# Rows and weight halves of a float32r streaming block at shifting SBUF addresses

## The chip, the cores and the metric

The kernel runs on one NeuronCore of a Trainium2 chip. The metric is the device time of one execution in microseconds (us). Smaller is better.

## What is computed

A residual block over 272 tokens (16 learned ones and 256 of the input), model width 2048, in float32: a feed-forward part, a mixer part and a second feed-forward part, each between two RMSNorms.

```python
h = h + 0.5 * rmsnorm(swiglu(rmsnorm(h, g), w_gate, w_up, w_down), g2)   # 2048 -> 5632 -> 2048
u = rmsnorm(h, mix_pre_g)
z = u @ w_in + b_in                     # 2048 -> 10248 columns: q, k, v, gates, two sigmoid gates
y = sigmoid(gm) * (mlstm(...) @ m_w_branch) + sigmoid(ga) * (diff_attention(...) @ a_w_branch)
h = h + rmsnorm(y @ w_out, mix_post_g)
h = h + 0.5 * rmsnorm(swiglu(...), ...) # the second feed-forward part
return h[:, 16:]                        # the learned tokens are dropped
```

From the queries of the mixers on, only the 256 tokens of the input are carried along; the second feed-forward part works on 256 tokens.

## The kernel before

All weights stream through SBUF once. They lie in DRAM as 377 units (of 128 x 2048 float32, 1 MB); `load_unit` brings one by DMA into a tile `W` (three buffers) and splits it into a high part H, which ACT rounds to float32r, and a low part L = W - H, which DVE writes. H and L come in two halves of 1024 columns, with four buffers each, so two units are held at a time. Tokens are split the same way: the operand of a sub-layer lies in `U`, 16 rows of 576 elements for each partition, the high row first and the low row right behind it at `T` = 272 elements. The hidden activations of a feed-forward part lie in three slots `G0`, `G1`, `G2`.

A matrix product is then three matmuls in float32r, H·XH + H·XL + L·XH, and `product` issues them for one 128 x 128 piece of weights and one row `k`. There are four kinds of units. *Wide* ones work on 272 tokens, as three matmuls of 272 columns (a PSUM bank holds 512). *Narrow* ones work on 256 tokens: H·XH and H·XL go as one matmul of 512 columns whose moving operand is `both`, a pattern of two rows, and L·XH is one of 256. *Cells* are the rows of `G0` to `G2` with 272 tokens in the down projection of the first part, *dense* are those with 256 tokens in the second one and in the two branches. Where `both` is None (the first group of a part, the last block of a tensor that needs it, one of four banks at the end of a down projection), 256 tokens too run as three matmuls.

In products with `both`, `turn` flips from one product to the next, so that the order is both·L, L·both, both·L, L·both; at the first product of a sum it is set back, and the last product always ends with `both`. A kind's units are counted from 0 through the program. `block` runs the 16 rows of one block of 128 output columns; `group` runs four blocks at a time, row by row, over several units. The feed-forward parts are one group and the blocks of gate and up, a down projection over 24 of the 44 hidden blocks, the remaining blocks, and a down projection over the other 20.

Every kind has one fixed pair of starts inside its H and L buffers, in bytes:

```python
PHASES = {"wide": (192, 0), "narrow": (32, 96), "cells": (64, 64), "dense": (192, 192)}
hp, lp = [p // 4 for p in PHASES[kind]]
H = sp.tile([128, 1088], F32R, name="H", bufs=4)[:, hp:hp + 1024]
L = sp.tile([128, 1088], F32R, name="L", bufs=4)[:, lp:lp + 1024]
```

`ROW` is 576 and `CELL` 320 elements. Each engine takes its instructions in the order in which the program is written; nothing is scheduled afterwards. The functions that the diff touches, with the line numbers of the profile:

Of the kernel before, what the change touches and what calls it, by code (L numbers as in the profile page):

```python
# [22 lines left out]
F32R = mybir.dt.float32r  # L23
I32 = mybir.dt.int32
BF16 = mybir.dt.bfloat16
AF = mybir.ActivationFunctionType
OP = mybir.AluOpType
AX = mybir.AxisListType.X

D, SEQ, META, DFF = 2048, 256, 16, 5632  # L30
T = META + SEQ
KT = D // 128
FT = DFF // 128
FA = 24
FB = FT - FA
MH, DQK, DV = 4, 128, 256
AH, ADH, ADV = 8, 64, 128
# [3 lines left out]
ALL, REAL = slice(0, T), slice(META, T)  # L41
# [35 lines left out]
GAPS = (32, 40, 8)  # L77

PHASES = {"wide": (192, 0), "narrow": (32, 96), "cells": (64, 64), "dense": (192, 192)}

@with_exitstack
def block_kernel(ctx: ExitStack, tc: tile.TileContext, ht_d, w_d, vec_d, con_d, gc_d, out_d):
# [10 lines left out]
    def f(ap):  # L98
        return ap.bitcast(F32)
# [4 lines left out]

    hT = cp.tile([128, KT, T], F32, name="hT")
    gap(cp, 0)
    rows = cp.tile([128, KT, ROW], F32R, name="U")
    U = rows[:, :, :2 * T].rearrange("p k (a t) -> p k a t", a=2)
    UH, UL = U[:, :, 0], U[:, :, 1]
    A = cp.tile([128, 4352], F32, name="A")  # L110
    vec = cp.tile([128, NVEC], F32, name="vec")
    con = cp.tile([128, NCON], F32, name="con")
# [5 lines left out]
    def view(t, off, *shape):  # L118
        n = int(np.prod(shape))
        a = t[:, off:off + n]  # L120
        if len(shape) == 1:
            return a
        return a.rearrange("p (a b) -> p a b", a=shape[0])

    def slot(tag, n, dt):
        return gp.tile([128, n], dt, tag=tag, name=tag, bufs=1)

    def v(name, j, n=1):
        o, w = VEC[name]
        return vec[:, o + j:o + j + n]  # L130
# [4 lines left out]

    st = {"pieces": 2}
    unit_no = [0]
    turn = [False]

    def behind(ins, prev):  # L140
        tc.add_manual_dep(ins.ins, prev.ins.name,
                          mybir.DependencyInfo(mybir.DependencyClass.NoSync,
                                               mybir.DependencyReason.DATA), reason="issue order")

    def load_unit(kind, parts=1, hold=None, dma=None):
        pieces = max(parts, st["pieces"])
        u = unit_no[0]
        unit_no[0] += 1
        W = sp.tile([128, 2048], F32, name="W", bufs=3)
        hp, lp = [p // 4 for p in PHASES[kind]]  # L150
        n = 2048 // parts
        for i in range(parts):
            s = slice(i * n, (i + 1) * n)
            st["dma"] = nc.sync.dma_start(W[:, s], w_d[u, :, s])
            if dma:
                dma(i)
        HL = []
        for i in range(2):
            H = sp.tile([128, 1088], F32R, name="H", bufs=4)[:, hp:hp + 1024]
            L = sp.tile([128, 1088], F32R, name="L", bufs=4)[:, lp:lp + 1024]  # L160
            n = 2048 // pieces
            for o in range(0, 1024, n):
                s = slice(o, o + n)
                w = W[:, 1024 * i + o:1024 * i + o + n]
                a = nc.scalar.activation(H[:, s], w, AF.Copy)  # L165
                b = nc.vector.tensor_sub(L[:, s], w, f(H[:, s]))  # L166
                q = (1024 * i + o) // n
                if hold and hold[q % len(hold)]:
                    for x, y in zip((a, b), hold[q % len(hold)]):
                        behind(x, y)  # L170
            HL.append((H, L))
        return HL
# [26 lines left out]
        return tp.tile([128, n], dt, tag=f"s{n}", name=name, bufs=bufs)  # L199

    def product(ps, HL, o, X, first, last):
        turn[0] = False if first else not turn[0]
        H, L = HL[o // 1024]
        o %= 1024
        H, L = H[:, o:o + 128], L[:, o:o + 128]
        XH, XL, both = X
        n = XH.shape[-1]
        if both is None:
            nc.tensor.matmul(ps[:, :n], H, XH, start=first, stop=False)  # L209
            nc.tensor.matmul(ps[:, :n], H, XL, start=False, stop=False)  # L210
            st["mm"] = nc.tensor.matmul(ps[:, :n], L, XH, start=False, stop=last)  # L211
        elif last or turn[0]:
            nc.tensor.matmul(ps[:, :n], L, XH, start=False, stop=False)  # L213
            st["mm"] = nc.tensor.matmul(ps[:, :2 * n], H, both, start=False, stop=last)  # L214
        else:
            nc.tensor.matmul(ps[:, :2 * n], H, both, start=first, stop=False)  # L216
            st["mm"] = nc.tensor.matmul(ps[:, :n], L, XH, start=False, stop=False)  # L217
# [100 lines left out]
        return ps  # L318

    def prenorm_operand(k, g, cols):  # L320
        a = nc.scalar.activation(UH[:, k, cols], hT[:, k, cols], AF.Copy, scale=v(g, k))  # L321
        b = nc.vector.scalar_tensor_tensor(UL[:, k, cols], hT[:, k, cols], v(g, k),  # L322
                                           f(UH[:, k, cols]), op0=OP.mult, op1=OP.subtract)
        return a, b

    def operand(cols):
        return [(UH[:, k, cols], UL[:, k, cols], U[:, k, :, cols]) for k in range(KT)]

    def residual(yg, r, cols, n, g):
        def feed(k):  # L330
# [33 lines left out]
    def ffn(cols, n, post, feed):  # L364
        Y = view(A, 0, KT, n)
        cells, F = [], []
        for tag in SLOTS:
            w = CELL if n > 256 else n
            m = SLOTS[tag] // w if n > 256 else 2 * (SLOTS[tag] // (2 * n))
            t = view(slot(tag, SLOTS[tag], F32R), 0, m, w)  # L370
            cells += [t[:, i, :n] for i in range(m)]
            F += [(t[:, i], t[:, i + 1], t[:, i:i + 2]) for i in range(0, m - 1, 2)]
        X = operand(cols)
        if n > 256:
            F = [(cells[i], cells[FA + i], None) for i in range(FA)]
            X = plain(X)
        state = {}

        def gate(ps):
            t = tmp()  # L380
            times(t[:, :n], ps, state["r"][:, :n])
            nc.scalar.activation(t[:, :n], t[:, :n], AF.Silu)
            return t

        def up(j, sg, ps):
            t = tmp()
            times(t[:, :n], ps, state["r"][:, :n])
            nc.vector.tensor_mul(t[:, :n], t[:, :n], sg[:, :n])
            H, L, _ = F[j % FA]
            nc.scalar.activation(H, t[:, :n], AF.Copy)  # L390
            nc.vector.tensor_sub(L, t[:, :n], f(H))

        def pair(j):
            sg = gate(block(X, 8))
            up(j, sg, block(X, 8))

        def down(chunk, nk):
            for g in range(4):
                last = chunk == 1

                def finish(b, ps):
                    k = 4 * g + b
                    for p in ps:
                        nc.vector.tensor_add(Y[:, k], p, Y[:, k])
                    add_square(state["acc"], Y[:, k], n, k)
                    post_scale(Y, k, post)

                pss = group(F, nk, n, tail=last, after=finish if last else None)
                if not last:
                    for b in range(4):  # L410
                        total(Y[:, 4 * g + b], pss[b])

        psn[0] = 0
        pss = group(X, KT, n, feed=feed)
        pss += [block(X, 8) for _ in range(2)]
        state["r"] = rstd_of(prenorm_sum(cols, n), n, "rpre")
        pss.append(block(X, 8))
        sgs = [gate(pss[0]), gate(pss[1])]
        up(0, sgs[0], pss[2])
        up(1, sgs[1], pss[3])  # L420
        up(2, gate(pss[4]), pss[5])
        up(3, gate(pss[6]), block(X, 8))
        for j in range(4, FA):
            pair(j)
        down(0, FA)
        for j in range(FA, FT):
            pair(j)
        state["acc"] = []
        down(1, FB)
        r = rstd_of(state["acc"], n, "rpost")  # L430
        return Y, r
# [313 lines left out]
    wide = {"mq", "mk", "mv", "ak", "av"}  # L745

    XA, XR = plain(operand(ALL)), operand(REAL)
    waiting, units = [], []

    def start_block(i, cycle=1):  # L750
        full = IN_ORDER[i] == "if" or IN_ORDER[i][0] in wide
# [2 lines left out]
    def begin(g):  # L754
        if g is not None and next(g, "end") != "end":
            waiting.append(g)

    def advance():
        with tc.issue_after(st["mm"].ins):
            for g in list(waiting):  # L760
                if next(g, "end") == "end":
                    waiting.remove(g)
            if units:
                begin(units.pop(0))

    def run(i0, i1):
        for i in range(i0, i1):
# [10 lines left out]
    base = {k: IN_ORDER.index((k, 0)) for k in ("mv", "ak", "gm", "ga")}  # L778
    run(7, base["ak"])
    st["pieces"] = 4  # L780
    units += [mlstm(h, i) for i in range(2) for h in range(MH)]
    run(base["ak"], base["gm"])
    while waiting or units:
        advance()
    st["lam"] = lam()
    units += [attention(h, i) for i in range(2) for h in range(AH)]

    def keep(j, ps):
        total(tm[:, j], ps)
# [1 line left out]
    branch(HM, keep)  # L791
    gz = view(slot("G0", SLOTS["G0"], F32), 0, KT, SEQ)
    run(base["gm"], base["ga"])
    while waiting or units:
        advance()
    st["pieces"] = 2
    for j in range(KT):
# [9 lines left out]
    def merge(j, ps):  # L807
        t = tmp()
        times(t[:, :SEQ], ps, gz[:, j])
        nc.vector.tensor_add(t[:, :SEQ], t[:, :SEQ], tm[:, j])  # L810
        nc.scalar.activation(UH[:, j, REAL], t[:, :SEQ], AF.Copy)
        nc.vector.tensor_sub(UL[:, j, REAL], t[:, :SEQ], f(UH[:, j, REAL]))

    branch(HA, merge)

# [187 lines left out]
```

## Time and profile before

| | before |
|---|---|
| median of the runs | 2274.9 us (2 runs, 2274.74 to 2275.07) |
| profiled execution, its own time | 2273.81 us |
| span of its instructions | 2272.0 us |
| PE busy | 2254.3 us, 99% |
| PE weight loads busy | 2082.1 us, 92% |
| DVE busy | 1419.5 us, 62% |
| ACT busy | 1159.6 us, 51% |
| DMA | 404.56 MB, mean 178 GB/s |

Busy time is the union of an engine's records. Matmuls overlap each other in the records: the next one starts well before the one ahead has ended. So how fast PE goes is read from the distance of starts in the timeline, or from the number of records in a stretch, and not from the mean length of one. Each matmul has a weight load of its own (PEld), also where two in a row use the same weights.

### The profile page before, as it was taken

What the parts mean: (1) busy time and instruction counts of PE and PEld (TensorE: products, weight loads), DVE (VectorE), ACT (ScalarE), POOL (GpSimd) and SP (SyncE); (2) the same over time, 40 slices, a digit from 0 to 9 for tenths busy, and PEclk for the clock granted to TensorE, in tenths of its full rate; (3) what the DMA queues carried; (4) which work ended last, traced back from release to release, by engine and by line L of the source; (5) the groups of instructions that cost most, each with busy time, mean ns of one, the idle gap of its engine ahead of it and who ended that gap; (6) DMA issues with size and microseconds to landing.
All of it is one profiled execution on the core that took longest, in us unless ns stands there. A gap on an engine that the chain in (4) does not pass through costs nothing.

```text
span 2272.0 us, 37068 instructions
## 1 busy us (share of the span) xinstructions
PE 2254.3 (99%) x15325; PEld 2082.1 (92%) x15325; DVE 1419.5 (62%) x2470; ACT 1159.6 (51%) x1869; POOL 0.8 (0%) x5
## 2 busy tenths in 40 slices
PE   9999999999999999999999999999999999999998
PEld 9999999999999998988988888888888888888897
DVE  7555544455555596588588758668666545666655
ACT  6444433444444465555569655556555444545443
POOL 0000000000000000000000000000000000000000
PEclk9999999999999999999999999999999999999999
DMA  7545554554545544434433555545555555555553
GB/s 257 181 179 181 173 185 173 180 180 174 185 171 182 201 158 167 167 131 163 169 135 130 188 195 189 188 167 186 186 185 187 195 194 185 187 193 195 186 185 111
DMA packets 61529, 404.56 MB, mean 178 GB/s; under 512 B 6704, under 2 KB 8880, under 8 KB 14000
## 3 DMA queue, kind: packets, MB, share of 16 engines
q1 hardware_dynamic: 61216, 400.33, 49.6%
q8 instruction: 120, 1.97, 0.3%
q0 software_dynamic: 144, 1.87, 0.2%
q14 instruction: 49, 0.40, 0.0%
HBM read 400.07 MB, written 2.10 MB: 177 GB/s over the span
## 4 chain that ended last, share of the span: by engine, by line
PE 98%; DVE 1%; DMA 0%; ACT 0%; issue 0%; SPq 0%; DVEq 0%
PE mm L214 10%; PE mm L216 10%; PE mm L211 7%; PE mm L209 7%; PE mm L210 7%; PE aux L211 6%; PE aux L209 6%; PE aux L210 6%; PE aux L214 5%; PE aux L216 5%; PE mm L213 5%; PE mm L217 5%; PE aux L213 3%; PE aux L217 3%; PE vt L211 2%; PE vt L209 2%
## 5 line engine op out<-in xcount | busy, mean ns | idle before, releaser
L166 DVE TENSOR_TENSOR L<-W,H 128x1024 fp32r<-128x1024 f32 (+1 forms) x866 | 934.9, 1085 | 597.0 <-ACT H L165 586.6
L165 ACT ACTIVATE H<-W 128x1024 fp32r<-128x1024 f32 (+1 forms) x866 | 811.9, 946 | 751.7 <-PE aux L210 209.3
L209 PE MATMUL mm<-U,H 128*128 128x272 f32 (+1 forms) x1056 | 304.4, 289 | 8.3 <-ACT U L321 7.9
L211 PE MATMUL mm<-U,L 128*128 128x272 f32 (+1 forms) x1056 | 303.6, 288 | 0.4 <-DVE L L166 0.4
L210 PE MATMUL mm<-U,H 128*128 128x272 f32 (+1 forms) x1056 | 302.3, 287 | 0.2 <-DVE U L322 0.2
L216 PE MATMUL mm<-U,H 128*128 128x512 f32 x728 | 288.0, 396 | 0.0
L214 PE MATMUL mm<-U,H 128*128 128x512 f32 x728 | 286.7, 394 | 0.0
L211 PE MATMUL aux<-U,L 128*128 128x272 f32 x752 | 215.8, 287 | 0.0
L209 PE MATMUL aux<-U,H 128*128 128x272 f32 x752 | 214.8, 286 | 0.0
L210 PE MATMUL aux<-U,H 128*128 128x272 f32 x752 | 214.3, 285 | 0.0
L209 PEld LDWEIGHTS mm<-U,H 128*128 128x128 f32 x1056 | 199.5, 189 | 10.3 <-ACT U L321 9.2
L217 PE MATMUL mm<-U,L 128*128 128x256 f32 x728 | 205.6, 282 | 0.0
L213 PE MATMUL mm<-U,L 128*128 128x256 f32 x728 | 203.4, 279 | 0.0
L211 PEld LDWEIGHTS mm<-U,L 128*128 128x128 f32 x1056 | 199.7, 189 | 0.9 <-DVE L L166 0.9
L210 PEld LDWEIGHTS mm<-U,H 128*128 128x128 f32 x1056 | 199.6, 189 | 0.8 <-DVE U L322 0.4
L213 PEld LDWEIGHTS mm<-U,L 128*128 128x128 f32 x728 | 137.1, 188 | 31.5 <-issue 0.4
L217 PEld LDWEIGHTS mm<-U,L 128*128 128x128 f32 x728 | 137.2, 189 | 30.5 <-issue 0.7
L216 PE MATMUL aux<-U,H 128*128 128x512 f32 x367 | 144.8, 395 | 0.0
L209 PEld LDWEIGHTS aux<-U,H 128*128 128x128 f32 x752 | 141.3, 188 | 0.1
L211 PEld LDWEIGHTS aux<-U,L 128*128 128x128 f32 x752 | 141.3, 188 | 0.0
L210 PEld LDWEIGHTS aux<-U,H 128*128 128x128 f32 x752 | 141.0, 188 | 0.1
L214 PE MATMUL aux<-U,H 128*128 128x512 f32 x353 | 138.7, 393 | 0.0
(272 smaller groups left out, 4408.2 us busy)
## 6 DMA issues: line engine op xcount, KB each, us to landing
W<-in_w_dram SPq DMA_DIRECT2D x369, 1024.0 KB, 4.8
W<-in_w_dram SPq DMA_DIRECT2D x32, 256.0 KB, 5.3
out_dram<-hT SPq DMA_DIRECT2D x8, 256.0 KB, 2.4
G<-in_gc_dram POOLq DMA_DIRECT2D x1, 1824.0 KB, 8.4
hT<-in_h_dram SPq DMA_DIRECT2D x6, 272.0 KB, 5.5
hT<-in_h_dram SPq DMA_DIRECT2D x1, 544.0 KB, 6.1
con<-in_con_dram SPq DMA_DIRECT2D x1, 528.0 KB, 5.8
vec<-in_vec_dram SPq DMA_DIRECT2D x1, 118.5 KB, 2.1
```

The source lines that it names most:

```text
L165: a = nc.scalar.activation(H[:, s], w, AF.Copy)
L166: b = nc.vector.tensor_sub(L[:, s], w, f(H[:, s]))
L209: nc.tensor.matmul(ps[:, :n], H, XH, start=first, stop=False)
L210: nc.tensor.matmul(ps[:, :n], H, XL, start=False, stop=False)
L211: st["mm"] = nc.tensor.matmul(ps[:, :n], L, XH, start=False, stop=last)
L213: nc.tensor.matmul(ps[:, :n], L, XH, start=False, stop=False)
L214: st["mm"] = nc.tensor.matmul(ps[:, :2 * n], H, both, start=False, stop=last)
L216: nc.tensor.matmul(ps[:, :2 * n], H, both, start=first, stop=False)
L217: st["mm"] = nc.tensor.matmul(ps[:, :n], L, XH, start=False, stop=False)
```

## The change

Low token rows no longer follow their high row at a fixed distance. In `U` it is 272 elements plus 8 times (k mod 5); for the cells the second cell starts 8·(i mod 7) elements later; the dense rows lie 576 elements apart and the low row stands at 256 plus 8·(i mod 8). In elements of 4 bytes, 8 elements are 32 bytes. The starts of H and L in their buffers are no longer fixed by kind: `phase` counts the units of each kind and goes through 32 pairs, 8·(i mod 8) elements for H and 8·((i + 2·(i div 8)) mod 8) for L. And `turn` flips as before in all units but narrow ones with (i div 32) odd, that is units 32 to 63 and 96 to 127 of 152: there every product but the last of a sum runs both·L. The number of instructions stays the same on every engine. The list `units` is renamed `starts`.

```diff
-PHASES = {"wide": (192, 0), "narrow": (32, 96), "cells": (64, 64), "dense": (192, 192)}
+def apart(kind, i):
+    return 8 * (i % {"rows": 5, "cells": 7, "dense": 8}[kind])
...
-    rows = cp.tile([128, KT, ROW], F32R, name="U")
-    U = rows[:, :, :2 * T].rearrange("p k (a t) -> p k a t", a=2)
-    UH, UL = U[:, :, 0], U[:, :, 1]
+    U = cp.tile([128, KT * ROW], F32R, name="U")
+
+    def twin(t, at, step, n):
+        both = None
+        if at + 2 * step <= t.shape[-1]:
+            both = t[:, at:at + 2 * step].rearrange("p (a b) -> p a b", a=2)[:, :, :n]
+        return t[:, at:at + n], t[:, at + step:at + step + n], both
+
+    def token_row(k, cols):
+        return twin(U, ROW * k + cols.start, T + apart("rows", k), cols.stop - cols.start)
...
+    units = {"wide": 0, "narrow": 0, "cells": 0, "dense": 0}
...
+    def phase(kind):
+        i = units[kind]
+        units[kind] += 1
+        st["turns"] = kind != "narrow" or i // 32 % 2 == 0
+        return 8 * (i % 8), 8 * ((i + 2 * (i // 8)) % 8)
...
-        hp, lp = [p // 4 for p in PHASES[kind]]
+        hp, lp = phase(kind)
...
-        turn[0] = False if first else not turn[0]
+        turn[0] = False if first else not turn[0] and st["turns"]
...
-            w = CELL if n > 256 else n
-            m = SLOTS[tag] // w if n > 256 else 2 * (SLOTS[tag] // (2 * n))
-            t = view(slot(tag, SLOTS[tag], F32R), 0, m, w)
-            cells += [t[:, i, :n] for i in range(m)]
-            F += [(t[:, i], t[:, i + 1], t[:, i:i + 2]) for i in range(0, m - 1, 2)]
+            t = slot(tag, SLOTS[tag], F32R)
+            if n > 256:
+                cells += [(t, CELL * i) for i in range(SLOTS[tag] // CELL)]
+            else:
+                F += [twin(t, ROW * i, SEQ + apart("dense", len(F) + i), n) for i in range(8)]
...
-            F = [(cells[i], cells[FA + i], None) for i in range(FA)]
+            for i in range(FA):
+                (t, a), (z, b) = cells[i], cells[FA + i]
+                b += apart("cells", i)
+                F.append((t[:, a:a + n], z[:, b:b + n], None))
```

On PE, at the step from narrow unit 31 to unit 32 (a block of the last mixer gate `ga`), the order before was this; the number behind `mm` names the block, those behind H and L the half of the weights:

```order
L213 MATMUL mm_14312<-U_72,L_14322 128x256
L214 MATMUL mm_14312<-U_72,H_14321 128x512
L216 MATMUL mm_14411<-U_72,H_14414 128x512
L217 MATMUL mm_14411<-U_72,L_14415 128x256
L213 MATMUL mm_14411<-U_72,L_14415 128x256
L214 MATMUL mm_14411<-U_72,H_14414 128x512
```

At the same place now (L226 and L228 are the two lines with `both`, L225 and L229 those with L):

```order
L225 MATMUL mm_14312<-U_72,L_14322 128x256
L226 MATMUL mm_14312<-U_72,H_14321 128x512
L228 MATMUL mm_14411<-U_72,H_14414 128x512
L229 MATMUL mm_14411<-U_72,L_14415 128x256
L228 MATMUL mm_14411<-U_72,H_14414 128x512
L229 MATMUL mm_14411<-U_72,L_14415 128x256
```

The second product of unit 32 has changed places with itself: H with both rows first and L behind it, as in the first product. Addresses, which the rest of the change is about, are not seen in such rows.

On DVE, at the first blocks of the mixer gate `ga` (narrow unit 32 and the next), with the semaphores that an instruction waits for in brackets, the order before was this (`A`, `G_13058` and `t` are sums and gates on their way out of PSUM):

```order
L166 TENSOR_TENSOR L<-W,H 128x1024 [waits Activation_49]
L799 TENSOR_TENSOR A<-A,G_13058 128x256 [waits Activation_49]
L166 TENSOR_TENSOR L<-W,H 128x1024 [waits DMAHW2_49,Activation_49]
L229 TENSOR_TENSOR t<-mm,t 128x256 [waits Activation_49]
L234 TENSOR_TENSOR t<-t,rpre 128x256 [waits DVE_49]
```

Now it is this:

```order
L178 TENSOR_TENSOR L<-W,H 128x1024 [waits Activation_49]
L815 TENSOR_TENSOR A<-A,G_13058 128x256 [waits Activation_49]
L178 TENSOR_TENSOR L<-W,H 128x1024 [waits DMAHW2_49,PE_49,Activation_49]
L241 TENSOR_TENSOR t<-mm,t 128x256 [waits Activation_49]
L246 TENSOR_TENSOR t<-t,rpre 128x256 [waits DVE_49]
```

The order is the same; the write of a unit's first half of L now waits for PE as well. 59 more writes of L than before do so.

## Rows read from the trace of the kernel before

**Rows 1.** The page, parts 1 and 2: engines, and granted clock in 40 slices.

```profile
PE 2254.3 (99%) x15325; PEld 2082.1 (92%) x15325; DVE 1419.5 (62%) x2470; ACT 1159.6 (51%) x1869; POOL 0.8 (0%) x5
...
PEclk9999999999999999999999999999999999999999
```

**Rows 2.** The page, part 4: the chain that ended last, by engine.

```profile
PE 98%; DVE 1%; DMA 0%; ACT 0%; issue 0%; SPq 0%; DVEq 0%
```

**Rows 3.** The waits of PE, whole span: total us, times, longest us.

```profile
PE mm L209 <- ACT U L321: 7.9, 2, 4.0
PE aux L317 <- DVE eps L435: 1.1, 1, 1.1
PE mm L845 <- DVE A L842: 1.0, 2, 0.8
PE mm L211 <- DVE L L166: 0.4, 2, 0.2
PE mm L209 <- ACT H L165: 0.3, 1, 0.3
```

**Rows 4.** Windows, PE: stretch, us, busy (records), granted clock, DMA share, GB/s.

```profile
300.00:430.00 130.00, 130.00 (x1056) 1.00 0.50 179
450.00:650.00 200.00, 200.00 (x1624) 1.00 0.50 179
...
1260.00:1375.00 115.00, 115.00 (x665) 1.00 0.55 192
...
1560.00:1770.00 210.00, 210.00 (x1202) 1.00 0.52 188
1930.00:2130.00 200.00, 200.00 (x1156) 1.00 0.53 190
1800.00:1920.00 120.00, 120.00 (x697) 1.00 0.53 192
2190.00:2250.00 60.00, 60.00 (x387) 1.00 0.40 144
```

**Rows 5.** Timeline, PE, narrow block: start us, length us, line, output<-inputs, shape.

```profile
1457.04 0.39 PE L216 MATMUL mm<-U,H 128*128 128x512 f32 x1
1457.27 0.28 PE L217 MATMUL mm<-U,L 128*128 128x256 f32 x1
1457.38 0.28 PE L213 MATMUL mm<-U,L 128*128 128x256 f32 x1
```

**Rows 6.** Timeline, PE's weight loads in the same stretch.

```profile
1457.04 0.19 PEld L217 LDWEIGHTS mm<-U,L 128*128 128x128 f32 x1
1457.27 0.19 PEld L213 LDWEIGHTS mm<-U,L 128*128 128x128 f32 x1
```

**Rows 7.** Timeline, PE, starts of two dense groups, four products each.

```profile
1790.04 0.40 PE L216 MATMUL mm<-G,H 128*128 128x512 f32 x1
...
1790.40 0.40 PE L216 MATMUL mm<-G,H 128*128 128x512 f32 x1
...
1790.75 0.39 PE L216 MATMUL mm<-G,H 128*128 128x512 f32 x1
...
1791.45 0.28 PE L213 MATMUL mm<-G,L 128*128 128x256 f32 x1
...
1856.40 0.39 PE L216 MATMUL mm<-G,H 128*128 128x512 f32 x1
...
1857.80 0.28 PE L213 MATMUL mm<-G,L 128*128 128x256 f32 x1
```

**Rows 8.** Timeline, PE, last block of the output projection: three matmuls a product.

```profile
1506.96 0.28 PE L209 MATMUL mm<-U,H 128*128 128x256 f32 x1
...
1512.26 0.28 PE L209 MATMUL mm<-U,H 128*128 128x256 f32 x1
```

**Rows 9.** The page, part 5: writes of L and H, busy us and mean ns.

```profile
L166 DVE TENSOR_TENSOR L<-W,H 128x1024 fp32r<-128x1024 f32 (+1 forms) x866 | 934.9, 1085 | 597.0 <-ACT H L165 586.6
L165 ACT ACTIVATE H<-W 128x1024 fp32r<-128x1024 f32 (+1 forms) x866 | 811.9, 946 | 751.7 <-PE aux L210 209.3
```

More of the change, by code (lines that the diff above doesn't have):

```diff
@@ L320, in prenorm_operand @@
     def prenorm_operand(k, g, cols):
-        a = nc.scalar.activation(UH[:, k, cols], hT[:, k, cols], AF.Copy, scale=v(g, k))
-        b = nc.vector.scalar_tensor_tensor(UL[:, k, cols], hT[:, k, cols], v(g, k),
-                                           f(UH[:, k, cols]), op0=OP.mult, op1=OP.subtract)
+        H, L, _ = token_row(k, cols)
+        a = nc.scalar.activation(H, hT[:, k, cols], AF.Copy, scale=v(g, k))
+        b = nc.vector.scalar_tensor_tensor(L, hT[:, k, cols], v(g, k), f(H), op0=OP.mult,
+                                           op1=OP.subtract)
         return a, b
     def operand(cols):
-        return [(UH[:, k, cols], UL[:, k, cols], U[:, k, :, cols]) for k in range(KT)]
+        return [token_row(k, cols) for k in range(KT)]
     def residual(yg, r, cols, n, g):
@@ L747, in block_kernel @@
     XA, XR = plain(operand(ALL)), operand(REAL)
-    waiting, units = [], []
+    waiting, starts = [], []
     def start_block(i, cycle=1):
@@ L762, in advance @@
                     waiting.remove(g)
-            if units:
-                begin(units.pop(0))
+            if starts:
+                begin(starts.pop(0))
     def run(i0, i1):
@@ L780, in block_kernel @@
     st["pieces"] = 4
-    units += [mlstm(h, i) for i in range(2) for h in range(MH)]
+    starts += [mlstm(h, i) for i in range(2) for h in range(MH)]
     run(base["ak"], base["gm"])
-    while waiting or units:
+    while waiting or starts:
         advance()
     st["lam"] = lam()
-    units += [attention(h, i) for i in range(2) for h in range(AH)]
+    starts += [attention(h, i) for i in range(2) for h in range(AH)]
     def keep(j, ps):
@@ L793, in block_kernel @@
     run(base["gm"], base["ga"])
-    while waiting or units:
+    while waiting or starts:
         advance()
@@ L810, in merge @@
         nc.vector.tensor_add(t[:, :SEQ], t[:, :SEQ], tm[:, j])
-        nc.scalar.activation(UH[:, j, REAL], t[:, :SEQ], AF.Copy)
-        nc.vector.tensor_sub(UL[:, j, REAL], t[:, :SEQ], f(UH[:, j, REAL]))
+        H, L, _ = token_row(j, REAL)
+        nc.scalar.activation(H, t[:, :SEQ], AF.Copy)
+        nc.vector.tensor_sub(L, t[:, :SEQ], f(H))
     branch(HA, merge)
```

## Prediction

> **What bounds the kernel now.** I read the page's engine table first. PE is busy for 99% of the span, DVE for 62% and ACT for 51%, and the granted clock stands in the top tenth in all 40 slices, 1.00 in every stretch that I took apart, which is the 2.4 GHz level [rows 1, 4]. The chain of work that ended last is 98% PE [rows 2]. A busy PE can still be a waiting one, so the waits come next: all that PE waited for is some 11 us of 2272, of which H and L account for 0.7 us [rows 3]. So PE is never short of work; the time is the number of its instructions times the pace at which they start. No share of busy time shows that pace, because a matmul's record is longer (0.28 or 0.39 us) than the distance to the next start (0.11 or 0.23 us) [rows 5].
>
> Take as the unit a product: one 128x128 piece of weights, split into H and L, times one k-row of tokens, split likewise: H·XH, H·XL, L·XH. With 272 tokens these are three matmuls of 272 columns. With 256 tokens they are one of 512 columns (H times both rows) and one of 256. From the loops, the first sort occurs 2640 times (2112 in the first feed-forward part, 33 blocks of 16 in the mixers), the second 3392 times (2112 in the second feed-forward part, 48 blocks of 16 and two branches of 128 in the mixers, 256 in the output projection).
>
> The pace follows from the stretches of [rows 4]: microseconds over products, a product being 2 records (3 in the wide stretches, 9 for 4 products in the last row, where every fourth runs as three matmuls), after taking off the 2 records that were still running at a stretch's start. 210/(1200/2) gives 350.0 ns, 200/(1154/2) 346.6, 120/(695/2) 345.3, 115/(663/2) 346.9, 60/(385·4/9) 350.6. The wide ones: 130/(1054/3) = 370.0 and 200/(1622/3) = 369.9. By stage the 3392 cost 704·350.0 (gate and up blocks, first part) + 640·346.6 (second part) + 384·345.3 + 320·350.6 (the two down groups) + 64·353.3 [rows 8] + 1280·346.9 = 1179.7 us, 347.8 each; the 2640 cost 976.8 us at 370.0. These 2156 us are 95% of the span.
>
> What matters for this change is that 350.0 and 346.6 come from the same instructions at the same addresses: gate and up blocks of one feed-forward part, before and after the first down group. So the pace is not fixed by the instructions alone. Each matmul comes with a weight load of its own, which starts with the matmul before it [rows 5, 6]; so two read streams always run side by side, and they settle into a pattern that repeats every two or four products and then holds for 200 us. There are better and worse such patterns: 345.3 and 350.6 are 1.5% apart.
>
> **The change, part by part.**
>
> *Addresses.* No instruction is added. Before, 576, 320 and 1088 elements of 4 bytes are 9, 5 and 17 times 256 bytes, so all rows and weight halves of one kind stand at one place modulo 256. Now the low row moves by 0 to 4 steps of 32 bytes from k to k (0 to 6 for the cells, 0 to 7 for the dense rows), and the starts of H and L go through 32 pairs, a new one with every unit, that is every 5.5 to 5.9 us. A pattern that repeats over two or four products no longer meets the same addresses again, so I expect none to hold. What an unsettled stream costs is shown by three places. At the start of a dense group the products run in another order: four in 1.41 us and four in 1.40, 351 ns each [rows 7]. Where one of four runs as three matmuls: 350.6 [rows 4]. Where all run as three: 15 in 5.30 us, 353.3 [rows 8]. Their mean is 351.7. I take 351.5 for the 256-token products: +3.7·3392 = +12.6 us. For the wide ones no such row exists. The same share would make 370.0 into 373.9, +10.3 us; all wide stretches, under two different pairs of starts, lie within 0.1 ns of each other, which speaks for no effect. I take half, +5.2 us. The ends: below, everything at the best pace that was held, 345.3, and the wide ones less by the same 0.7%: -2.5·3392 - 2.7·2640 = -15.6 us. Above, everything at the slowest single product, 0.36 us from 1790.04 to 1790.40 [rows 7], and the wide ones by that 3.5%: +12.2·3392 + 13·2640 = +75.7 us.
>
> *Order.* In narrow units 32 to 63 and 96 to 127 H and L no longer swap places from product to product. That is 63 units of 16 products (the last unit of the output projection runs as three matmuls in both kernels), 1008 in all. The nearest row is again the start of a dense group, where both·L·both·L stands already: 351 against 345.3 in the swapped order right after it [rows 4, 7]. Alone it would cost between 0 and 5.7·1008 = +5.7 us. The 351.5 above is already the price of an unsettled stream, so I don't add it.
>
> *A wait.* In these units the first half's last reader is the L matmul, so the write of the next L into that buffer waits for PE itself, where the wait of H before it had covered it: 59 more such writes. Behind it on DVE's queue stand the next L and the sums out of PSUM. The wait ends one matmul later than the one of ACT for the same half, 0.12 us [rows 5], and the half is wanted only after the unit in between, some 5.5 us. Writing takes 0.95 us on ACT and 1.09 us on DVE [rows 9]. I cost it at nothing; if that cover were gone, 59·0.12 = 7 us would be the most.
>
> *DVE and ACT* write H and L to shifted starts. They are idle for 38% and 49% of the span [rows 1], so even 10% longer writes, 0.1 us each, stay covered. The gated rows of the second feed-forward part go 8 to a slot where 9, 9 and 6 stood before: same instructions, nothing to wait for.
>
> The sum is +17.8 us on the profiled execution's 2273.8 us, 2291.6; the median of the runs is 1.1 us above that execution, so 2293 us.
>
> The Trainium skill speaks against any effect. "SBUF — State Buffer", section "Who interferes with whom", has two independent read ports for PE, one for the moving rows and one for weight loads, and says that PE and ACT never wait on anyone. "TensorE: Matmul & The Clock Gate", section "Back-to-back issue gap", gives N/2.4 + 2.5 ns, 215.8 + 109.2 = 325 ns for a product of 512 and 256 columns wherever they stand, and the sum would be 0. The trace disagrees in size: 345.3 to 350.6, and two paces for the same instructions.
>
> **The rivals.**
>
> *Addresses are indifferent* (0.24). PE's stream is slowed by something that does not see 32-byte steps, and the two paces come from how a stretch began. For it: the wide stretches, with starts of 192 and 0 in one kind and 64 and 64 in the other, differ by 0.1 ns. Against it: the dense pace of 345.3 and the narrow one of 346.6 to 350.0, same columns, other starts. Then only the order counts, 0 to 5.7 us: 2275 to 2281. The two sections of the Trainium skill named above would give this.
>
> *Mixing frees the stream from a bad pattern* (0.13). If the held patterns of 350.0 are the accident, and streams that shift all the time collide less, all goes towards 345.3 and its share of the wide: -15.6 us, 2259. For it: 704 products sit in the bad pattern for 230 us. Against it: none of the three unsettled places is faster than 350.
>
> *Some pairs of starts collide throughout* (0.21, the slower side). Moving rows and weight loads are then in step at the same place for a whole unit, as in the first product of the dense group (0.36 us) [rows 7], and one part of the 32 pairs pays that for all 16 products. At the mean of the first two there, 0.355, it is +7.2·3392 and 2.1% of the wide, +45 us, 2320; at 0.36 it is 2350; its middle is 2332. It decides from +7.5 ns a product on, which is 2%.
>
> **How the numbers follow.** The forecast has 0.42 (2281 to 2315), the rivals 0.24, 0.13 and 0.21. The range of 2260 to 2332 takes in the forecast, the indifferent addresses, most of the faster case and half of the slower one; some 0.05 is left out below and 0.12 above. Two per cent, about what a measurement of this kernel can tell from no change, is 45.5 us. To be faster by that, a product would have to lose 7.5 ns, which puts the narrow ones at 340, below the best pace held anywhere: 0.02. Slower by over 2% has most of the last rival, 0.20. Within 2%: 0.78.
>
> **What would show it.** In the profile of the changed kernel PE should still be 99% busy with waits near 11 us. Taking the stretches of [rows 4] again, the pace should lie near 351 in all narrow stages alike, with single starts that no longer repeat from product to product but change from unit to unit; 346 to 350 with clean repeats would mean that addresses are indifferent. If the pace changes with the pair of starts and comes back after 32 units, the collision is real; if the wide stages move more than the narrow ones, I sized them wrongly. Units with the fixed order should be at most 6 ns a product slower than the others. If PE begins to wait for H or L, the added wait was not free, and the prediction is wrong in a way that I left out.

## The result, and the profile after

The changed kernel takes 2300.3 us against 2274.9, a ratio of 1.0115 with a 95% interval of 1.0097 to 1.0132. It is 25.4 us slower, where the forecast said 18. The page of the changed kernel, engines, granted clock, and the chain that ended last by engine, reads like [rows 1, 2]:

```profile
PE 2279.6 (99%) x15325; PEld 2102.2 (91%) x15325; DVE 1420.5 (62%) x2470; ACT 1160.3 (50%) x1869; POOL 0.8 (0%) x5
...
PEclk9999999999999999999999999999999999999999
...
PE 98%; DVE 1%; DMA 0%; ACT 0%; issue 0%; SPq 0%; DVEq 0%
```

The same instructions, the same clock, PE 25.3 us longer busy. What PE waits for (total us, times, longest us) stands beside [rows 3]:

```profile
PE mm L221 <- ACT U L334: 7.9, 2, 4.0
PE mm L221 <- ACT H L177: 1.1, 1, 1.1
PE aux L329 <- DVE eps L451: 1.1, 1, 1.1
PE mm L862 <- DVE A L859: 1.0, 2, 0.8
PE mm L223 <- DVE L L178: 0.2, 1, 0.2
```

11.3 us in all, and 0.2 us for L: the added waits of DVE reach nobody. So the loss lies in the pace, and the windows view of the changed kernel gives it stage by stage, as [rows 4] did (cells, wide, narrow mixers, first gate and up, first dense group, second gate and up):

```profile
305.00:435.00 130.00, 130.00 (x1038) 1.00 0.49 176
455.00:655.00 200.00, 200.00 (x1595) 1.00 0.49 174
1275.00:1390.00 115.00, 115.00 (x657) 1.00 0.53 189
1580.00:1800.00 220.00, 220.00 (x1257) 1.00 0.53 188
1822.00:1940.00 118.00, 118.00 (x677) 1.00 0.53 189
1955.00:2160.00 205.00, 205.00 (x1173) 1.00 0.53 189
```

Less the 2 records in flight, these are 376.4, 376.6, 351.1, 350.6, 349.6 and 350.1 ns a product, against 370.0, 369.9, 346.9, 350.0, 345.3 and 346.6. Wide products lost 6.6 ns, those with 256 tokens lost 2.6 on the mean (350.4 against 347.8 over all their starts): 2640·6.6 + 3392·2.6 = 26.2 us, close to the 25.9 by which the span grew.

The pace changes from unit to unit and comes back. In the changed kernel's timeline these are the first matmuls of wide units 30 and 31, and of 62 and 63:

```profile
188.45 0.28 PE L221 MATMUL aux<-U,H 128*128 128x272 f32 x1
...
194.41 0.29 PE L221 MATMUL aux<-U,H 128*128 128x272 f32 x1
...
525.85 0.28 PE L221 MATMUL aux<-U,H 128*128 128x272 f32 x1
...
531.81 0.29 PE L221 MATMUL aux<-U,H 128*128 128x272 f32 x1
```

5.96 us for 16 products both times, 373 ns, the fastest of the 32 pairs; the slowest takes 379. So the stream is not restless. A unit's pace comes back with its addresses 32 units on, and what the pace answers to is what the experiments are about.

### The profile page after: what moved, and what is told of

It is laid out like the page before. It is cut to its first block, busy times and chain, and to the rows that moved or that the text cites. A ratio compares the mean times of both kernels' runs of the same rounds, so it can differ in the third digit from the quotient of the medians.

```text
span 2297.9 us, 37068 instructions
## 1 busy us (share of the span) xinstructions
PE 2279.6 (99%) x15325; PEld 2102.2 (91%) x15325; DVE 1420.5 (62%) x2470; ACT 1160.3 (50%) x1869; POOL 0.8 (0%) x5
## 4 chain that ended last, share of the span: by engine, by line
PE 98%; DVE 1%; DMA 0%; ACT 0%; issue 0%; SPq 0%; DVEq 0%
PE mm L228 12%; PE mm L222 7%; PE mm L221 7%; PE mm L223 7%; PE mm L226 7%; PE mm L229 6%; PE aux L221 6%; PE aux L228 6%; PE aux L222 6%; PE aux L223 6%; PE aux L226 4%; PE mm L225 4%; PE aux L229 3%; PE aux L225 2%; PE vt L228 2%; PE vt L222 2%
## 5 line engine op out<-in xcount | busy, mean ns | idle before, releaser
L228 PE MATMUL mm<-U,H 128*128 128x512 f32 x1015 | 377.7, 397 | 0.0
L229 PE MATMUL mm<-U,L 128*128 128x256 f32 x1015 | 285.3, 281 | 0.0
L221 PE MATMUL aux<-U,H 128*128 128x272 f32 x752 | 217.3, 289 | 0.0
L222 PE MATMUL aux<-U,H 128*128 128x272 f32 x752 | 216.5, 288 | 0.0
L228 PEld LDWEIGHTS mm<-U,H 128*128 128x128 f32 x1015 | 191.5, 189 | 26.6 <-issue 1.1
L229 PEld LDWEIGHTS mm<-U,L 128*128 128x128 f32 x1015 | 191.5, 189 | 19.6 <-issue 0.7
L221 PEld LDWEIGHTS mm<-U,H 128*128 128x128 f32 x1056 | 199.3, 189 | 10.7 <-ACT U L334 9.2
L222 PEld LDWEIGHTS mm<-U,H 128*128 128x128 f32 x1056 | 200.0, 189 | 0.9 <-DVE U L335 0.5
L223 PEld LDWEIGHTS mm<-U,L 128*128 128x128 f32 x1056 | 199.8, 189 | 0.8 <-DVE L L178 0.8
L228 PE MATMUL aux<-U,H 128*128 128x512 f32 x479 | 179.1, 394 | 0.0
L226 PE MATMUL mm<-U,H 128*128 128x512 f32 x441 | 175.3, 398 | 0.0
L229 PE MATMUL aux<-U,L 128*128 128x256 f32 x479 | 134.3, 280 | 0.0
L225 PE MATMUL mm<-U,L 128*128 128x256 f32 x441 | 124.5, 282 | 0.0
```

## The experiments

Diffs are against the changed kernel. `PHASES`, with the fixed pairs of before, comes back where it is named. Unit paces are read from the first starts of units, as just shown.

**The three parts one by one.** Pairs alone:

```diff
-    return 8 * (i % {"rows": 5, "cells": 7, "dense": 8}[kind])
+    return 0
-        st["turns"] = kind != "narrow" or i // 32 % 2 == 0
+        st["turns"] = True
```

> Only the starts of H and L go through the 32 pairs; the low rows stand at their old distance and the order flips everywhere. If the cost comes from breaking a pattern that holds (my theory), a unit's 16 products repeat with one pair, the stream settles again within a few products, and little is left: 2275 to 2283 us. If the pair itself sets the pace, nearly all of the +25 us stays, 2293 to 2300, the wide units run at 374 to 379 ns a product as they do in the changed kernel, and the paces come back after 32 units.

2299.4 us, 1.0111 (1.0096 to 1.0126): nearly the whole loss. First starts of wide units 13, 14 and 15 in its timeline, and of 46 and 47:

```profile
87.01 0.29 PE L221 MATMUL aux<-U,H 128*128 128x272 f32 x1
...
93.00 0.28 PE L221 MATMUL aux<-U,H 128*128 128x272 f32 x1
...
98.93 0.29 PE L221 MATMUL aux<-U,H 128*128 128x272 f32 x1
...
285.48 0.28 PE L221 MATMUL aux<-U,H 128*128 128x272 f32 x1
...
291.41 0.29 PE L221 MATMUL aux<-U,H 128*128 128x272 f32 x1
```

Unit 13 takes 5.99 us, 374.4 ns a product, and unit 14 takes 5.93 us, 370 ns, as does unit 46, 32 units on. Unit 14 has the pair (192, 0), the one that wide units had before. The pair sets the pace, and my theory of a broken pattern fails here: within a unit nothing but the pair is new. A unit also settles soon: the products of wide unit 76 take 381, 379 and 374 ns, and the other 13 take 380 each.

Rows alone:

```diff
-        st["turns"] = kind != "narrow" or i // 32 % 2 == 0
-        return 8 * (i % 8), 8 * ((i + 2 * (i // 8)) % 8)
+        st["turns"] = True
+        return tuple(p // 4 for p in PHASES[kind])
```

> Only the distance of the low rows changes with k; the starts of H and L are fixed by kind as before and the order flips everywhere. If breaking the pattern costs, this has nearly all of it: 2293 to 2300 us, wide products near 376 ns. If the pairs set the pace, 2275 to 2281 us, wide products at 370 to 371 ns.

2293.9 us, 1.0088 (1.0073 to 1.0103). Its windows over cells, wide products and the first gate and up stage:

```profile
310.00:430.00 120.00, 120.00 (x965) 1.00 0.49 176
450.00:650.00 200.00, 200.00 (x1601) 1.00 0.50 176
1580.00:1790.00 210.00, 210.00 (x1202) 1.00 0.54 189
```

373.8, 375.2 and 350.0 ns. By the expectation this spoke for the broken pattern: single wide products take 371 to 380 ns. But whole units repeat (375.4 ns a product in every wide unit from 7 to 87 but number 48, which starts a stage), and 1.0111 and 1.0088 do not add up to the 1.0115 of both, so each alone already takes the streams away from where they stood.

Order alone (fixed pairs, `apart` returning 0, the line with `turns` as in the change):

> Only the order in the narrow units 32 to 63 and 96 to 127. By the forecast's term between 0 and +5.7 us: 2275 to 2281 us, the units with the fixed order at up to 351 ns a product. If the order has no price of its own, 2275 us, and at most the unlucky pattern at 350 ns a product moves to other stretches.

2273.9 us, 0.9998 (0.9989 to 1.0008). The order has no price. Windows over narrow units 72 to 95, which flip, and 96 to 111, which do not:

```profile
1560.00:1700.00 140.00, 140.00 (x803) 1.00 0.52 188
1705.00:1785.00 80.00, 80.00 (x463) 1.00 0.54 191
```

350 and 347 ns: the fixed order even left the slower of the two patterns.

**Distances changed, but alike for all rows:**

```diff
-    return 8 * (i % {"rows": 5, "cells": 7, "dense": 8}[kind])
+    return 16
```

with the fixed pairs and the order of before. (At this distance the row k = 15 no longer fits the pattern of two rows and runs as three matmuls, 147 products, some 0.4 us.)

> All low rows stand 64 bytes further from their high rows, for every k alike, pairs fixed and order as before. If what counts is that the stream repeats, a pattern holds again, with single starts that repeat every two to four products, and the time is 2275 us, 10 us more or less. If the distance itself matters, the kinds move apart: wide products at 374 to 379 ns and 2290 to 2300 us, or as much faster.

2300.4 us, 1.0116 (1.0101 to 1.0131). Windows over wide, cells, wide and narrow products:

```profile
100.00:290.00 190.00, 190.00 (x1502) 1.00 0.48 172
310.00:430.00 120.00, 120.00 (x967) 1.00 0.49 178
450.00:670.00 220.00, 220.00 (x1754) 1.00 0.49 173
1580.00:1800.00 220.00, 220.00 (x1296) 1.00 0.53 188
```

380.0, 373.1, 376.7 and (33 records for 16 products) 350.7 ns. Here everything repeats again: wide units keep 380.0 from number 7 on through the first stage, and 376.7 in the second. A pattern that holds is as slow as one that doesn't. My theory falls.

**A second theory: the pace hangs on where the moving rows and the weight halves stand against each other, and each kind stood at a rare good place.** It has two sharp tests, both at the old distances of the low rows and in the old order. Rows and pairs of the wide and narrow products all move by 64 bytes:

```diff
-        return twin(U, ROW * k + cols.start, ...)
+        return twin(U, ROW * k + 16 + cols.start, ...)
+PHASES = {"wide": (256, 64), "narrow": (96, 160), "cells": (64, 64), "dense": (192, 192)}
```

> All token rows of the wide and narrow products and both starts of their pairs move by the same 64 bytes; distances of low rows and the order as before; cells and dense rows untouched. If the pace hangs on where the two read streams stand against each other, nothing changes: 2274 us, wide products at 370.0 ns, narrow ones at 346.6 to 350.0. If it hangs on where the weight halves lie by themselves, the wide pair (256, 64) should run like (0, 64) in the run of the 32 pairs, 380 ns, and the narrow one like (96, 160), 349.2: about 2295 us.

And only the rows move (the pairs of before stay):

> The token rows of the wide and narrow products move by 64 bytes, the pairs stay. If the streams' places against each other decide, this is the old rows with pairs 64 bytes lower, (128, 192) and (224, 32): by the run of the 32 pairs 379.6 ns for the wide and 347.1 for the narrow products, so 2292 us with all of the loss in the wide stages. If only the weight halves' own places count, 2274 us and 370.0 ns.

The first takes 2273.5 us, 0.9994 (0.9985 to 1.0003); its windows over wide, first and second gate and up products give 370.0, 346.5 and 346.6 ns:

```profile
450.00:650.00 200.00, 200.00 (x1624) 1.00 0.50 179
1560.00:1770.00 210.00, 210.00 (x1214) 1.00 0.53 189
1930.00:2130.00 200.00, 200.00 (x1156) 1.00 0.54 190
```

The second takes 2295.3 us, 1.0089 (1.0075 to 1.0102). Cells, wide, first and second gate and up:

```profile
310.00:430.00 120.00, 120.00 (x975) 1.00 0.51 180
450.00:650.00 200.00, 200.00 (x1582) 1.00 0.49 174
1580.00:1790.00 210.00, 210.00 (x1202) 1.00 0.53 187
1960.00:2150.00 190.00, 190.00 (x1098) 1.00 0.53 189
```

370.0 for the untouched cells, 379.7 for the wide (379.6 was expected from the pairs), 350.0 and 346.7 for the narrow, as before. So moving rows and halves together by 64 bytes does nothing, and for the wide products their place against each other is what counts. For the narrow ones the second test says little, since the pair that they come to was expected to cost nothing.

One rival is left: the rows have also moved against the places where ACT and DVE write the next H and L. The trace of the rows-only run decides it. A stretch without ACT and DVE (in the columns us, PE, PEld, DVE, ACT, POOL, granted clock, DMA share, GB/s), and the first matmuls of two products around it, three products apart:

```profile
606.07:606.78 0.71, 0.71 (x7) 0.71 (x7) 0.00 (x0) 0.00 (x0) 0.00 (x0) 1.00 1.01 427
...
605.90 0.29 PE L224 MATMUL mm<-U,H 128*128 128x272 f32 x1
...
607.04 0.29 PE L224 MATMUL vt<-U,H 128*128 128x272 f32 x1
```

1.14 us, 380 ns a product, and in that trace all 527 products from 450 to 650 us take 380 ns, whether ACT and DVE are busy or idle. Their writes are not the cause.

**All pairs.** Rows as before, and the 32 pairs that the change leaves out (`i + 1 + 2 * (i // 8)` in `phase`):

> Rows as before, and the 32 pairs of starts that the changed kernel leaves out, L at an odd number of 32-byte steps from H. If each kind's fixed pair of before is a rare good place, all of these are worse: 2295 to 2305 us, wide units at 373 to 380 ns, narrow at 347 to 354. If odd distances are something else, a unit kind runs below its pace before (370.0, 346.6, 345.0), and a better pair can be read off.

2300.8 us, 1.0116 (1.0101 to 1.0132). Both runs of pairs give this map of the wide products, in ns, read once a stage has settled:

```
start of H     0     32     64     96    128    160    192    224   L behind H, modulo 256
           377.1  374.4  373.6  376.5  376.8  374.0  373.8  373.3     0
           379.1  371.7  379.0  373.4  379.4  376.9  379.9  373.4    32
           380.2  377.5  377.6  376.6  379.6  374.6  370.1  377.8    64
           374.1  373.2  373.6  377.1  375.8  377.9  378.2  373.6    96
           377.5  377.6  373.0  377.7  378.5  377.2  373.3  373.6   128
           376.9  373.2  375.4  374.1  377.6  376.4  373.5  378.2   160
           379.6  377.9  373.8  375.3  374.8  376.1  375.2  375.3   192
           379.7  378.8  373.4  377.7  380.0  375.4  373.8  376.7   224
```

The pair of before, H at 192 and L 64 behind it, is the one place near 370; the next best is 371.7. It is so for the cells too (370.2 at (64, 64), next 372.1), and the best dense unit (344.9) and one of the two best narrow ones (346.8) have the pairs of before. An entry is not the pair alone: every pair comes after the same one each time, and at the start of a stage the same pair can run otherwise, (0, 64) at 375.1 in unit 8 and 380.2 in units 40 and 72. So an entry has to be tested by holding the pair.

With the wide low half at byte 256 instead of 0 (fixed pairs, else as before):

> Only the wide units' low half moves, from byte 0 to byte 256 of its buffer; all else as before the change. If places count modulo 256 bytes, nothing changes: 2274 us, wide products at 370.0 ns. If they count modulo something larger, the wide products leave that pace, for 373 to 380 ns and 2282 to 2300 us.

2274.5 us, 1.0001 (0.9991 to 1.0011), and as many records from 450 us on as before:

```profile
450.00:650.00 200.00, 200.00 (x1624) 1.00 0.49 179
```

For these halves 256 bytes are a full turn.

Two looks for better places, one execution each: starts half a step off (`4 + 8 * (i % 8), 4 + 8 * ((i + i // 8) % 8)`),

> Rows and order as before; the starts of H and L go through 64 pairs that all lie half a step, 16 bytes, beside those tried so far. If the good places are as rare and as narrow as the runs of the pairs suggest, every pair is worse than each kind's pair of before: 2290 to 2305 us, wide units at 372 to 381 ns, narrow at 347 to 356. If 32 bytes was too coarse a step, some units run below 370.0, 346.6 or 345.0.

2299.1 us; the best units reach 372.9 (wide), 370.1 (cells), 346.6 (narrow) and 346.9 ns (dense): for cells and narrow as good as before, none better. (Cells met 44 of the 64 pairs and dense units 60, here and in the next run.) And low rows 32 bytes further (`apart` returns 8), 64 pairs:

> All low rows stand 32 bytes further from their high rows, and the starts go through all 64 pairs in steps of 32 bytes. If each distance of the low row has a good pair of its own, one or two units in 64 of each kind run as fast as before (wide at 370, narrow at 347) and the rest at 372 to 380 and 347 to 356: 2290 to 2305 us in all. If the old distance is itself the good place, no pair comes below 373 for the wide units. A pair below 370.0 or 346.6 would be a better place than that of before.

2299.6 us. No wide pair comes below 373.2 and no cell below 371.3, so for the wide products, which met all 64 pairs, the old distance is itself part of the good place. But two narrow pairs, (128, 32) and (0, 32), run faster than anything before. Products 2 and 14 of narrow unit 108, pair (128, 32):

```profile
1790.23 0.39 PE L228 MATMUL aux<-U,H 128*128 128x512 f32 x1
...
1794.35 0.39 PE L228 MATMUL aux<-U,H 128*128 128x512 f32 x1
```

4.12 us for 12 products, 343.3 ns.

**A faster version.** First the fixed order in all narrow units, at the addresses of before (`st["turns"] = kind != "narrow"`, fixed pairs, `apart` 0):

> Addresses of before, and the fixed order in all narrow units instead of two groups of 32. In the run of the order alone the units 96 to 111 went from 350.0 to 346.7 ns a product. If the fixed order keeps the stream out of the slower of its two patterns, the 44 blocks of the first gate and up stage gain 3.3 ns on 704 products: 2.3 us, 2271.8 us. If that was an accident of where the stage began, 2274 us, one us more or less, with 350.0 somewhere else.

2272.5 us, 0.9992 (0.9983 to 1.0001). By time alone that is not clear; its trace has 1214 records where [rows 4] have 1202, 346.5 ns instead of 350.0:

```profile
1560.00:1770.00 210.00, 210.00 (x1214) 1.00 0.53 188
```

That the order did this is not shown: in the run with rows and pairs moved the same stage ran at 346.5 in the flipping order. Then with the better place from the output projection on, and the fixed order in the mixers alone:

```diff
+PHASES = {..., "far": (128, 32)}
-        return twin(U, ROW * k + cols.start, T + apart("rows", k), cols.stop - cols.start)
+        return twin(U, ROW * k + cols.start, T + st.get("far", 0), cols.stop - cols.start)
+        st["turns"] = kind != "narrow" or "far" in st
+        return tuple(p // 4 for p in PHASES["far" if kind == "narrow" and "far" in st else kind])
...
     run(base["ga"], NBLK)
+    st["far"] = 8
+    XR = operand(REAL)
```

> A version built from the readings: addresses of before up to the mixers, with the fixed order in their narrow units; from the output projection on, low rows 32 bytes further from the high ones and the narrow pair (128, 32), with the flipping order, which ran at 343.3 ns a product once settled in two units of the run of the 64 pairs. If a held pair keeps that pace, 704 products gain 6.7 ns, 640 gain 3.3 and 240 gain 3.4, 7.6 us, and the mixers some 0.5 us: 2266 us. If the pace was owed to the units around, 2272 to 2275 us, with 346 to 350 ns a product in the last part.

2266.8 us, 0.9969 (0.9957 to 0.9981): faster than both kernels. Its windows over wide, first and second gate and up products give 369.9, 343.1 and 343.1 ns:

```profile
450.00:650.00 200.00, 200.00 (x1624) 1.00 0.51 179
1560.00:1770.00 210.00, 210.00 (x1226) 1.00 0.54 191
1930.00:2130.00 200.00, 200.00 (x1168) 1.00 0.53 190
```

## Why the prediction was right, and where it was not

**The bound** was right: PE 99% busy, waits of 11.3 us, and the whole difference in its pace. Reading the pace from records in a stretch, not from their length, was what showed where the time went.

**Addresses** were the term that decided, and its sign was right; its mechanism was not. "I expect none to hold" fails: with all rows shifted alike a pattern held at 380.0 ns, and with one pair a unit settled within three products. In its place stands the position of the two streams against each other. Each kind had the best of the 64 pairs for its rows, or one level with the best, and shifting the pairs or the rows gives this up. Either alone costs 20 to 25 us, and both together no more. By the prediction's own sign, a pace that changes with the pair and comes back after 32 units, this is its last rival and not its forecast.

**The sizes** came near by luck, from two errors that partly cancel. For the 256-token products the rows of the trace before gave +3.7 ns, measured 2.6: +8.8 us instead of +12.6. Two of these rows did not even show what they were taken for. Where one product in four runs as three matmuls the stream of before is settled, as the first matmuls of dense units 41, 42 and 43 show:

```profile
2150.20 0.28 PE L213 MATMUL mm<-G,L 128*128 128x256 f32 x1
...
2155.80 0.28 PE L213 MATMUL mm<-G,L 128*128 128x256 f32 x1
...
2161.40 0.28 PE L213 MATMUL mm<-G,L 128*128 128x256 f32 x1
```

5.60 us a unit, 350.0 ns, and the same four products over and over (350, 343, 353, 354 ns). The row of 353.3 repeats too, from its third product on. They price other instructions and not an unsettled stream.

For the wide products I halved +10.3 us to +5.2, because two kinds with different pairs agreed at 370.0 within 0.1 ns; measured +17.4 us. That was the term that was sized wrongly, and the sign named for it, wide stages that move more than the narrow ones, came. The agreement did not show that addresses don't matter. The cells with their pair and the wide rows with theirs had each been at their own best place, and two best places look alike. A range of paces cannot be read from two points that both lie at its lower end.

Nor is two per cent what a measurement here can tell from no change: the interval of 1.0097 to 1.0132 leaves no doubt of the loss.

**Order**, taken as 0 with 5.7 us as its upper end: 0.9998, so 0. The row that I had for it was 351 ns at the starts of dense groups; in the narrow units the same order ran at 347. What makes those starts slow is not shown. **The wait**, taken as 0: PE waits 0.2 us for L in all. **DVE and ACT** at shifted starts: DVE's busy time 1420.5 us against 1419.5 [rows 1].

**The rivals.** "Addresses are indifferent" is refuted by one move: 64 bytes for the rows alone take the wide products from 370.0 to 379.7. The two sections of the Trainium skill behind it ("Who interferes with whom" in "SBUF — State Buffer" and "Back-to-back issue gap" in "TensorE: Matmul & The Clock Gate") have no term for this, and here the measurement decides. N/2.4 + 2.5, which the prediction set against the trace, is in the second of them the figure for an isolated matmul, not for a stream of weight loads and matmuls, so its 325 ns says little of this stream. "Mixing frees the stream from a bad pattern" has a true half: the pattern at 350.0 can be left, as two runs at 346.5 show, but mixing finds no better one; the changed kernel runs that stage at 350.6. "Some pairs collide throughout" is nearest to what happens, with one correction: it is not some pairs that are bad. In the wide products 63 of 64 are slower than that of before, by 0.4 to 2.7%.

**Open.** Which reads of the two streams meet is not shown, nor that reads meet at all; shown is that the pace follows their places. If only L against the low row counted, moving the low row up by 64 bytes would be the pair (192, 192), 373.8 ns in the map; measured were 380.0 and 376.7. Nor is it settled why the same addresses hold two paces, 350.0 and 346.6, or 380.0 and 376.7.

## What to carry to other kernels

When PE never waits, its pace may still hang on where the operands lie. Count starts in a steady stretch, and let one run go through all starts, unit by unit: the pace of each is in one trace, at a tenth of a per cent, where the time gives only their sum. Such a survey run is itself slow, since it gives up every good place; its use is the table that it leaves, and what is read from it has to be held in a run of its own.

## What the runs showed of the hardware

- The float32r matmul stream here, with one weight load per matmul, changed its pace by up to 3% (370.0 to 380.2 ns for three matmuls of 272 columns) with 32-byte steps of its operands in SBUF, at a clock of 1.00 throughout.
- What counted was the place of rows and weights against each other (2273.5 us with both moved by 64 bytes, 2295.3 with the rows alone); 256 bytes more for the wide low half changed nothing (2274.5). Writes of ACT and DVE did not change the pace (380 ns a product with and without them).
- At one and the same place the stream held one of two paces for 100 us and more (350.0 and 346.6 ns).
